# A hybrid decoder layer: the softmax attention's gate projected ahead of the linear attention's values, output sums begun with the softmax attention's part

## The chip, the cores and the metric

One core of a Trainium2 chip runs the whole program. The metric is the device time of one execution in microseconds (us); of several runs the median is given.

## The reference

One decoder layer for 512 prompt tokens and 8 sample tokens (one new token each of 8 running sequences), model width 1024. One input projection `h = x @ w_in` gives nine groups of columns; two mixers work on them side by side:

```python
qa, ka, va, za, ga, qb, kb, vb, gb = split(x @ w_in)      # 256 256 512 16 512 | 512 512 512 512
o_a = gated_linear_attention(qa, ka, va, decay(za))       # 4 heads, state 64 x 128, chunk-wise
o_a = rms_norm(o_a) * gla_norm_g
o_b = dilated_attention(qb, kb, vb, rel_bias)             # 8 heads of 64; windows (128,1),(512,4),(2048,16)
mix = concatenate([o_a * silu(ga), o_b * silu(gb)])       # 512 columns of part a, 512 of part b
y   = mix @ w_out
x_new = layer_norm(ALPHA * x + y) * ln_g + ln_b
```

Sample tokens do the same, with a given state for the linear attention and 1024 cached rows of keys and values each for the softmax attention. Everything is float32. The outputs are the new x, the states and the key and value rows.

## The kernel before, in words

**Numbers.** Each large product is taken as three matmuls of rounded halves: hi·hi, hi·lo, lo·hi (`three`). So each weight group is loaded raw, cast to its half hi on ScalarE (ACT), and subtracted to lo on VectorE (DVE); in the trace these are hi_vb, lo_vb and so on. The names end in parts: `lo1_vb1` is the lo half of load 1 of the second vb group.

**The projections.** The generator `dense()` writes TensorE's (PE) main stream: the projections in the order ka, za, qa, qb, kb, vb, va, ga, gb, and then the output projection. Groups of w_in are 128 columns wide (feature-major result, `feature`) or 256 wide (token-major result, `token`, for vb and va). The list `names` (L493) sets the order in which weights are loaded; the order of the code in `dense()` sets that of the matmuls. Tokens stand as four tiles of 128; u = 0 and 1 are the two halves of 256 tokens, and the first half also carries the 8 sample tokens (264 columns).

**The softmax attention (b).** For each head h and token tile the scores land in banks ps_s (`scores`); `softmax` adds the bias strip and takes the row maximum on DVE (`pr<-ps_s,strip`), the exponential on ACT, the division, then transposes the probabilities on PE into a bank ps_pt, from which ACT writes the half pth and DVE the half ptl (both are `pt` for the first token half). `weighted` multiplies them with the values (vhl) into a bank ps_pv; ACT copies half of it to pvl, and DVE adds both to obT, the output of two heads. Scores need q and k, so they run while vb is projected; products need vb as well.

**The sample tokens of b.** Their logits and probabilities (p_s) are made in small rows; psd_s is a scratch array in DRAM, from which the probabilities come back broadcast as pb. GpSimd (POOL) multiplies the cached values vv by pb, and DVE sums them (`o_pv<-vv`, eight times, once for each sample token).

**Gates and mixing.** `gate_into` takes a gate's projection in its bank through ACT (Exp, Ln, Exp into sg) and one DVE product, `ga<-ps_ga,sg` or `gb<-ps_gb,sg`. `mix_b` multiplies gb by obT and splits the product into mhb (ACT) and mlb (DVE). `mix_a` transposes the linear attention's output on PE into ps_oat, multiplies it with ga (`ga<-ps_oat,gn,ga`) and splits it into mha and mla. `mix_sample` does both for the 8 sample columns.

**The output projection.** `out_first` computes the first token half with the weights stationary, in units of 128 output columns (ps_yf): the first three units all do their k tiles 0 to 3 (part a) first and then 4 to 7 (part b), the other five run one by one. `out_turn` transposes the results back. `out_unit` does the second half (ps_y). Then come residual and LayerNorm.

**What sets the order.** Each task is a Python generator with a priority. `Plan.run` picks, by estimated costs, the operation that can start earliest (the lower priority number at a tie), and writes it to its engine; so the program is one fixed list for each engine, and each engine works its list in order. An operation of a task also waits in the planner for marks (`At`), for slots of a kind (`Need`, table SLOTS, L58) and for PSUM banks (BANKS, L67: d 3 for projections, s 3 for scores, t 2 for transposes). Slots that matter here: g (large tiles, 27), r (raw weights, 2), t1 (4; pvl, sg and other small tiles), ob (5; obT, which may also take a t1 slot as a spare). DMAs go over SyncE's (SP) queue in the order of its list. Each instruction is recorded at L359, in `Plan.issue`, so the profile is read by tile names.

Of the kernel before, what the change touches and what calls it, by code (L numbers as in the profile page):

```python
# [20 lines left out]
P = 128  # L21
# [40 lines left out]
    pt=4,  # L62
    t2=3, st=3,
    pr=4,
    t1=4, ob=5,
    m=6)
BANKS = dict(d=3, s=3, t=2)  # L67

# [295 lines left out]
def trunk(ctx: ExitStack, tc: tile.TileContext, xT, xp, xs, state, ck, cv, w_in, wab, gnorm,  # L364
# [81 lines left out]
    class Group:  # L446
# [11 lines left out]

        def load(self, i):
            raw = yield Need("r", f"raw{i}_{self.name}", [P, self.kk, self.w])  # L460
            rows = self.src[i * self.kk * P:(i + 1) * self.kk * P, self.c0:self.c0 + self.w]
            yield D.dma_start(raw, rows.rearrange("(k p) n -> p k n", p=P))
            raws.append((self, i, raw))
            mark("raw")
# [25 lines left out]
    def w_group(name, i, width=P):  # L490
        return Group(w_in, OFF[name] + i * width, f"{name}{i}_", width)

    names = [("ka", 2, P), ("qa", 2, P), ("qb", 4, P), ("kb", 4, P), ("vb", 2, GW), ("va", 2, GW), ("ga", 4, P), ("gb", 4, P)]  # L493
    groups = {f"{n}{i}": w_group(n, i, w) for n, c, w in names for i in range(c)}
    wo = [Group(w_out, g * 512, f"wo{g}_", 512) for g in range(2)]
    order = [g for k, g in groups.items() if k not in ("ka0", "ka1")] + wo
# [161 lines left out]
    def into(key, own, m, scale):  # L658
# [5 lines left out]
            mark(f"{key}_done")  # L664
        return evac

    def dense():
        for _ in range(N_WARM):
            yield T.matmul(warm_ps, warm[:, :P], warm, start=True, stop=True)
        free(warm_ps)  # L670
        free(warm)

        pk = {}
        for i in range(2):
            for u in range(2):
# [24 lines left out]
        for x in ("qh0", "ql0", "qh1", "ql1"):  # L700
            yield from make(x, Need("g", x, [P, 4, 256], F32R), 4)
        for i in range(4):
            yield from feature(groups[f"qb{i}"], parts("q", q_s, i, 0.125))
        for i in range(4):
            yield from make(f"kp{i}", Need("g", f"kp{i}", [P, 2, 512], F32R), 2)
            yield from feature(groups[f"kb{i}"], parts("k", k_s, i, 1.0))
        for i in range(2):
            for u in range(2):
                yield from make(f"vhl{i}{u}", Need("g", f"vhl{i}{u}", [P, 2, 4, 2, 64], F32R))
            yield from token(groups[f"vb{i}"], *vb_into(i))  # L710
        for u in range(2):
            yield from make(f"va{u}", Need("g", f"va{u}", [P, 2, 512]))
        for i in range(2):
            yield from token(groups[f"va{i}"], *va_into(i))
        for n, own in (("ga", ga_s), ("gb", gb_s)):
            for u in range(2):
                yield from make(f"{n}{u}", Need("g", f"{n}{u}", [P, 4, 256]))
            for i in range(4):
                yield from feature(groups[f"{n}{i}"], gate_into(n, own, i))
        free(*xt)  # L720
        for t in range(TT):
            add(residual(t), 8)
        add(residual_sample(), 8)
        units = [(g, f) for g in range(4) for f in range(2)]
        yield from out_first(*units[:3])
        for x in units[3:]:
            yield from out_first(x)
        for t, c, w in ((2, 0, 512), (2, 512, 512), (3, 0, 512), (3, 512, GW), (3, 768, GW)):
            yield from out_unit(t, c, w)
# [439 lines left out]
    def weighted(h, pi):  # L1169
# [4 lines left out]
            yield At(f"vb{h // 4}{i}", 2)  # L1174
        pth, ptl = B[f"pth{h}{pi}"], B[f"ptl{h}{pi}"]
        if h % 2 == 0:
            yield from make(f"obT{pi}{m}", Need(("ob", "t1"), f"obT{pi}{m}", [P, 256], spare=2))
        else:
            yield At(f"obT{pi}{m}")
        pv = yield bank(("s", "t"), f"ps_pv{h}{pi}")  # L1180
# [230 lines left out]
        if plan.marks[f"mix_b{u}"] == 4:  # L1411
            free(B[f"gb{u}"])

    def mix_sample():
        yield At("ga_s", 4)
        yield At("o_as")
        yield At("mla0")
        gas = ga_s.rearrange("p h b -> p b h")
        yield V.scalar_tensor_tensor(gas, o_as.rearrange("p (b h) -> p b h", h=HA), gn, gas, op0=ALU.mult, op1=ALU.mult)
        yield from split(ga_s, B["mha0"][:, :, GW:], B["mla0"][:, :, GW:])  # L1420
        mark("mix_s")
        yield At("gb_s", 4)
        yield At("o_bs")
        yield At("mlb0")
        yield V.tensor_tensor(gb_s, gb_s, o_bs, op=ALU.mult)
        yield from split(gb_s, B["mhb0"][:, :, GW:], B["mlb0"][:, :, GW:])
        mark("mix_s")


    def ln_rows():  # L1430
# [17 lines left out]
    def out_unit(t, c, w):  # L1448
        u, tl, cs = t // 2, slice((t % 2) * P, (t % 2) * P + P), slice(c % 512, c % 512 + w)
        g = wo[c // 512]  # L1450
        ps = yield bank("d", f"ps_y{t}{c // GW}")
        for k in range(KT):
            yield g.at(k)
            yield At(f"mix_a{u}", t % 2 + 1) if k < 4 else At(f"mix_b{u}{k - 4}")
            mh, ml = (B[f"m{x}{'ab'[k // 4]}{u}"][:, k % 4, tl] for x in "hl")
            hi, lo = g.hi[k][:, cs], g.lo[k][:, cs]
            yield from three(ps[:, :w], k, ((mh, hi), (mh, lo), (ml, hi)))
        add(out_evac(t, c // GW, ps[:, :w]), 2)

    def out_first(*units):  # L1460


        ps = []
        for g, f in units:
            ps.append((yield bank("d", f"ps_yf{g}{f}")))
            yield from out_half(g, f, ps[-1], range(4))
        for (g, f), p in zip(units, ps):
            yield from out_half(g, f, p, range(4, KT))
            add(out_turn(g, f, p), 2)

    def out_half(g, f, ps, ks):
        w, c = wo[g // 2], g % 2 * GW + f * P
        for k in ks:
            yield w.at(k)
            yield At("mix_a0", 2) if k < 4 else At(f"mix_b0{k - 4}")
            yield At("mix_s", 1 + k // 4)
            mh, ml = (B[f"m{x}{'ab'[k // 4]}0"][:, k % 4, :] for x in "hl")
            hi, lo = w.hi[k][:, c:c + P], w.lo[k][:, c:c + P]
            yield from three(ps[:, :TW[0]], k, ((hi, mh), (lo, mh), (hi, ml)))

# [105 lines left out]
    add(sample_v(vnt, "vnt", by_tile(vw_s)), 12)  # L1586
    add(sample_v(vat, "vat", by_tile(vad)), 12)
    add(sample_gla(), 11)
    add(mix_sample(), 16)
    add(ln_rows(), 17)  # L1590
    add(keys_store(), 17.5)
    for pi in range(2):
# [107 lines left out]
```

## Time and profile before

| | us |
|---|---|
| three runs | 293.41, 294.40, 294.72 |
| median | 294.4 |
| the profiled execution | 294.9 |
| its span on the core | 293.1 |
| granted clock of TensorE, mean | 0.984 |

The span is the time from the first to the last instruction that the trace shows. Before about 104 us the projections of ka to kb run; the vb projection and the first products of the softmax attention stand at 104 to 137, the rest of the softmax attention with va and the linear attention beside it at 137 to 202, the gates at 183 to 236, and the output projection from 236 on. A window's row gives, for each engine, its busy us and its instructions in that stretch. A wait `A tile <- B tile` says that engine A stood until B's instruction had written that tile.

### The profile page before, as it was taken

How to read it: one execution, taken by the hardware profiler on the slowest of the kernel's cores; microseconds unless marked ns; L12 is line 12 of the kernel's file. 1: busy time of each engine (PE TensorE's matmuls, PEld its weight loads, DVE VectorE, ACT ScalarE, POOL GpSimd, SP SyncE). 2: the span in 40 equal slices, each digit the busy share in tenths (PEclk: the TensorE clock that was granted, in tenths of full speed). 3: DMA queues.
4: the chain of work that ended last, by engine and by line, in shares of the span. 5: the costliest groups of instructions: out<-in, count | busy, mean ns of one | idle time of the engine just before them, and what ended most of it. 6: DMA issues, size and time to landing. Idle time of an engine off the chain costs nothing.

```text
span 293.1 us, 6910 instructions
## 1 busy us (share of the span) xinstructions
PE 276.3 (94%) x2636; PEld 260.4 (89%) x2636; DVE 228.7 (78%) x562; ACT 167.6 (57%) x463; POOL 57.3 (20%) x74
## 2 busy tenths in 40 slices
PE   7999999999999996999989899998999999999990
PEld 3899999998999995999978799998999999997880
DVE  4746897999799959679869877889899875339855
ACT  4747565356648756466857751789779964111100
POOL 4000001000872238000335535210410000000000
PEclk9999999999999999899999999999999999999996
DMA  6976422236967798148988967924954688650311
GB/s 189 289 199 183 130 74 73 75 83 201 308 189 208 243 246 269 41 129 218 251 187 199 275 161 209 238 75 137 290 151 144 202 269 266 115 173 26 121 74 72
DMA packets 58935, 51.18 MB, mean 175 GB/s; under 512 B 12554, under 2 KB 50196, under 8 KB 58902
## 3 DMA queue, kind: packets, MB, share of 16 engines
q1 hardware_dynamic: 58794, 50.66, 61.4%
q8 instruction: 21, 0.34, 0.5%
q14 instruction: 12, 0.10, 0.1%
q10 hardware_dynamic: 108, 0.07, 0.1%
HBM read 45.17 MB, written 6.03 MB: 175 GB/s over the span
## 4 chain that ended last, share of the span: by engine, by line
PE 71%; DVE 14%; DMA 6%; ACT 5%; issue 2%; SPq 0%; DVEq 0%; ACTq 0%
PE ps_yf L359 8%; PE ps_qb L359 8%; PE ps_gb L359 8%; PE ps_y L359 8%; PE ps_kb L359 4%; DMA strip<-tabr 4%; PE ps_qa L359 4%; PE ps_vb L359 4%; PE ps_vb_f L359 3%; PE ps_ka L359 3%; PE ps_ga L359 3%; DMA x_raw<-in_xT_dram 2%; PE ps_l L359 2%; PE ps_pv L359 2%; PE ps_va L359 2%
## 5 line engine op out<-in xcount | busy, mean ns | idle before, releaser
L359 POOL TENSOR_TENSOR vv<-vv,pb 128x256 f32<-128x256 f32 x32 | 27.9, 901 | 68.0 <-DMA pb<-psd_s 58.7
L359 POOL TENSOR_TENSOR past<-past,qbc 128x256 f32<-128x256 f32 x32 | 25.2, 820 | 43.1 <-DMA past<-in_ck_dram 37.5
L359 ACT ACTIVATE pr<-pr,ms 128x128 f32<-128x128 f32 (+3 forms) x49 | 26.0, 547 | 7.6 <-DVE ms L359 7.2
L359 PE MATMUL ps_pt<-cf,pr 128*128 128x128 f32 x80 | 14.5, 281 | 2.7 <-DVE pt L359 2.3
L359 DVE CUSTOM_DVE_ANT_0 pr<-ps_s,strip 128x128 f32<-128x128 f32 (+3 forms) x32 | 14.2, 478 | 1.0 <-DMA strip<-tabr 1.0
L359 PE MATMUL ps_ka<-xx,hi_ka 128*128 128x264 f32 (+1 forms) x64 | 12.6, 291 | 1.2 <-DVE xx L359 0.7
L359 ACT ACTIVATE sg<-sg 128x264 f32<-128x264 f32 (+1 forms) x32 | 13.3, 416 | 0.5
L359 PEld LDWEIGHTS ps_pt<-cf,pr 128*128 128x128 f32 x80 | 9.4, 142 | 3.7 <-DVE pt L359 2.7
L359 PEld LDWEIGHTS ps_ka<-xx,hi_ka 128*128 128x128 f32 x64 | 10.0, 188 | 2.5 <-DVE xx L359 1.1
L359 ACT COPY feat_y<-ps_yf 128x256 f32<-128x256 f32 x8 | 3.0, 373 | 15.2 <-PE ps_yf L359 15.2
L359 ACT ACTIVATE d<-d 128x512 f32<-128x512 f32 x13 | 7.8, 637 | 6.7 <-DVE d L359 6.7
L359 DVE TENSOR_TENSOR ptl<-ps_pt,pth 128x384 fp32r<-128x384 f32 (+1 forms) x16 | 9.6, 616 | 0.6 <-ACT pth L359 0.6
L359 ACT ACTIVATE rstd<-mv 128x1 f32<-128x1 f32 x4 | 0.7, 199 | 16.3 <-DVE mv L359 16.3
L359 POOL MEMSET att<- 64x512 f32 x2 | 1.0, 522 | 44.8 <-DVE ks L359 44.8
L359 DVE TENSOR_REDUCE o_pv<-vv 128x4 f32<-128x1024 f32 x8 | 9.7, 1209 | 0.0
L359 DVE TENSOR_REDUCE lt<-past 128x16 f32<-128x1024 f32 x8 | 9.6, 1202 | 0.0
L359 DVE TENSOR_TENSOR pt<-ps_pt,pt 128x128 fp32r<-128x128 f32 (+1 forms) x16 | 5.4, 347 | 5.3 <-ACT pt L359 5.3
L359 ACT CAST pth<-ps_pt 128x384 fp32r<-128x384 f32 (+1 forms) x16 | 8.4, 534 | 1.8 <-PE ps_pt L359 1.7
L359 DVE COPY lt<-ps_yf 128x8 f32<-128x8 f32 x6 | 1.0, 166 | 10.7 <-ACT feat_y L359 10.7
L359 PE MATMUL ps_ka<-xx,lo_ka 128*128 128x264 f32 (+1 forms) x32 | 9.1, 286 | 0.0
L359 ACT CAST pt<-ps_pt 128x128 fp32r<-128x128 f32 (+1 forms) x16 | 5.0, 317 | 6.8 <-PE ps_pt L359 6.6
L359 DVE TENSOR_TENSOR d<-b 128x1024 f32<-128x1024 f32 x7 | 8.5, 1217 | 0.0
(536 smaller groups left out, 1105.1 us busy)
## 6 DMA issues: line engine op xcount, KB each, us to landing
past<-in_ck_dram SPq DMA_DIRECT2D x8, 512.0 KB
vv<-in_cv_dram SPq DMA_DIRECT2D x8, 512.0 KB
pb<-psd_s SPq DMA_DIRECT2D x16, 256.0 KB
qbc<-qsd SPq DMA_DIRECT2D x8, 256.0 KB
strip<-tabr SPq DMA_DIRECT2D x8, 256.0 KB
y<-in_xp_dram SPq DMA_DIRECT2D x4, 512.0 KB
x_raw<-in_xT_dram SPq DMA_DIRECT2D x7, 260.0 KB
out_dram<-y SPq DMA_DIRECT2D x3, 512.0 KB
```

Source lines behind the costliest of these rows:

```text
L359: getattr(eng.eng, op.fn)(*op.args, **op.kw)
```

## The change

Five things are changed; what is computed is the same.

1. Slots: t1 has 6 instead of 4, ob 4 instead of 5, and obT takes only ob slots.
2. The projections' order is ka, za, qa, qb, kb, vb, gb, va, ga: gb now stands ahead of va, ga last. The loads of the weights follow. mix_b's steps can so be taken as soon as a pair of heads has its obT.
3. Sums of the output projection begin with part b: k tiles 0 to 3 are now mix_b's, 4 to 7 mix_a's, and w_out's rows are loaded in that order.
4. `out_first` begins with five units of part b, not three of part a, and its banks may come from d or s.
5. `mix_sample` is cut in two, for a and for b.

```diff
-    t1=4, ob=5,
+    t1=6, ob=4,
...
-            rows = self.src[i * self.kk * P:(i + 1) * self.kk * P, self.c0:self.c0 + self.w]
+            k = (i * self.kk + KT // 2 * (self.src is w_out)) % KT
+            rows = self.src[k * P:(k + self.kk) * P, self.c0:self.c0 + self.w]
...
-    names = [... ("vb", 2, GW), ("va", 2, GW), ("ga", 4, P), ("gb", 4, P)]
+    names = [... ("vb", 2, GW), ("gb", 4, P), ("va", 2, GW), ("ga", 4, P)]
...
+    def gates(n, own):
+        for u in range(2):
+            yield from make(f"{n}{u}", Need("g", f"{n}{u}", [P, 4, 256]))
+        for i in range(4):
+            yield from feature(groups[f"{n}{i}"], gate_into(n, own, i))
...
+        yield from gates("gb", gb_s)
         for u in range(2):
             yield from make(f"va{u}", Need("g", f"va{u}", [P, 2, 512]))
         for i in range(2):
             yield from token(groups[f"va{i}"], *va_into(i))
-        for n, own in (("ga", ga_s), ("gb", gb_s)):
-            for u in range(2):
-                yield from make(f"{n}{u}", Need("g", f"{n}{u}", [P, 4, 256]))
-            for i in range(4):
-                yield from feature(groups[f"{n}{i}"], gate_into(n, own, i))
+        yield from gates("ga", ga_s)
...
-        yield from out_first(*units[:3])
-        for x in units[3:]:
+        yield from out_first(*units[:5])
+        for x in units[5:]:
             yield from out_first(x)
...
-            yield from make(f"obT{pi}{m}", Need(("ob", "t1"), f"obT{pi}{m}", [P, 256], spare=2))
+            yield from make(f"obT{pi}{m}", Need("ob", f"obT{pi}{m}", [P, 256]))
...
-            yield At(f"mix_a{u}", t % 2 + 1) if k < 4 else At(f"mix_b{u}{k - 4}")
-            mh, ml = (B[f"m{x}{'ab'[k // 4]}{u}"][:, k % 4, tl] for x in "hl")
+            yield At(f"mix_b{u}{k}") if k < 4 else At(f"mix_a{u}", t % 2 + 1)
+            mh, ml = (B[f"m{x}{'ba'[k // 4]}{u}"][:, k % 4, tl] for x in "hl")
...
-            ps.append((yield bank("d", f"ps_yf{g}{f}")))
+            ps.append((yield bank(("d", "s"), f"ps_yf{g}{f}")))
```

What this does to the engines' lists is seen at three places.

**VectorE while vb is projected.** The names: `pt4`, `pt5`, `pt6` are probabilities of heads 4 to 6 of the first token half, ps_pt their banks; `vhl01` takes the first vb group's result; `obT00` and `obT01` are outputs of heads 0 and 1 and of heads 2 and 3; ln_new, l32, prod and lt belong to the sample logits. Before:

```order
L359 TENSOR_REDUCE lt_82<-past5_1576 128x2x8
L359 TENSOR_TENSOR pt4_1742<-ps_pt41_1767,pt4_1742 128x2x128
L359 TENSOR_TENSOR lo1_vb1__1803<-raw1_vb1__1496,hi1_vb1__1802 128x512 x2
L359 TENSOR_TENSOR vhl01_1579<-ps_vb0_3_1762,vhl01_1579 128x4x64
L359 TENSOR_TENSOR pt5_1746<-ps_pt50_1793,pt5_1746 128x128
L359 TENSOR_TENSOR prod_1719<-q_rows_79,k_rows_1697 32x128
L359 TENSOR_TENSOR lo0_va0__1813<-raw0_va0__1613,hi0_va0__1812 128x512
L359 TENSOR_REDUCE ln_new_1834<-prod_1719 32x2
L359 TENSOR_TENSOR l32_1835<-ln_new_1834,sel_1677 32x64
L359 TENSOR_TENSOR lo0_va0__1813<-raw0_va0__1613,hi0_va0__1812 128x512
L359 TENSOR_TENSOR obT00_1722<-ps_pv00_1723,pvl00_1741 64x256
L359 TENSOR_TENSOR obT00_1722<-ps_pv10_1724,pvl10_1847 64x256
```

The same place now:

```order
L359 TENSOR_TENSOR obT00_1726<-ps_pv00_1727,pvl00_1748 64x256
L359 TENSOR_TENSOR obT01_1729<-ps_pv30_1731,pvl30_1767 64x256
L359 TENSOR_TENSOR vhl01_1579<-ps_vb0_2_1679,vhl01_1579 128x4x64
L359 TENSOR_TENSOR pt4_1749<-ps_pt40_1750,pt4_1749 128x128
L359 TENSOR_REDUCE lt_82<-past5_1576 128x2x8
L359 TENSOR_TENSOR pt4_1749<-ps_pt41_1779,pt4_1749 128x2x128
L359 TENSOR_TENSOR pt5_1754<-ps_pt50_1791,pt5_1754 128x128
L359 TENSOR_TENSOR lo1_vb1__1820<-raw1_vb1__1496,hi1_vb1__1819 128x512
L359 TENSOR_TENSOR vhl01_1579<-ps_vb0_3_1771,vhl01_1579 128x4x64
L359 TENSOR_TENSOR l32_1722<-ln_new_1721,sel_1677 32x64
L359 TENSOR_TENSOR obT00_1726<-ps_pv10_1728,pvl10_1753 64x256
L359 TENSOR_TENSOR pt5_1754<-ps_pt51_1812,pt5_1754 128x2x128
```

Two obT rows have moved ahead of the split of vb1, that split is cut in two halves with rows between, and the split of va0 is gone from here (that of gb0 comes some rows later).

**SyncE's queue after the sample probabilities.** `psd_s` holds them in DRAM, `vv` is the cached values of one sample token, `pb` its probabilities broadcast. Before:

```order
L359 DMA psd_s_90<-p_s_2050 64x256
L359 DMA vv0_2090<-in_cv_dram 128x1024
L359 DMA pb0_2100<-psd_s_90 64x4x256 x2
L359 DMA out_5_dram<-vb_raw_2135 128x256
L359 DMA raw1_va1__2152<-in_w_in_dram 128x4x256
L359 DMA vv1_2144<-in_cv_dram 128x1024
L359 DMA pb1_2177<-psd_s_90 64x4x256
L359 DMA raw0_ga0__2181<-in_w_in_dram 128x8x128
L359 DMA pb1_2177<-psd_s_90 64x4x256
L359 DMA strip51_2234<-tabr_87 128x1x512
```

The same place now:

```order
L359 DMA psd_s_90<-p_s_2034 64x256
L359 DMA vv0_2070<-in_cv_dram 128x1024
L359 DMA out_5_dram<-vb_raw_2094 128x256
L359 DMA pb0_2082<-psd_s_90 64x4x256 x2
L359 DMA vv1_2119<-in_cv_dram 128x1024
L359 DMA pb1_2129<-psd_s_90 64x4x256 x2
L359 DMA raw0_gb3__2152<-in_w_in_dram 128x8x128
L359 DMA out_5_dram<-vb_raw_2181 128x256
L359 DMA raw0_va0__2188<-in_w_in_dram 128x4x256
L359 DMA strip51_2212<-tabr_87 128x1x512
```

vv1 and pb1 have moved ahead of the raw weights that stood between.

**VectorE at the last gate.** `ga_s` and `gb_s` are the sample columns. Before:

```order
L359 TENSOR_TENSOR gb0_3237<-ps_gb3_0_3572,sg_3619 128x256
L359 TENSOR_TENSOR gb_s_86<-ps_gb3_0_3572,sg_3619 128x8
L359 TENSOR_TENSOR gb0_3237<-gb0_3237,obT03_2020 128x256
L359 SCALAR_TENSOR_TENSOR ga_s_85<-o_as_84,gn_68,ga_s_85 128x8x4
L359 TENSOR_TENSOR mlb0_3310<-gb0_3237,mhb0_3309 128x256
L359 TENSOR_TENSOR mla0_3212<-ga_s_85,mha0_3211 128x4x8
L359 TENSOR_TENSOR gb_s_86<-gb_s_86,vnt_80 128x32
L359 TENSOR_TENSOR lo0_wo1__3623<-raw0_wo1__3565,hi0_wo1__3622 128x512
```

The same place now:

```order
L359 TENSOR_TENSOR ga0_3115<-ps_ga3_0_3536,sg_3593 128x256
L359 TENSOR_TENSOR ga_s_85<-ps_ga3_0_3536,sg_3593 128x8
L359 SCALAR_TENSOR_TENSOR ga0_3115<-ps_oat_3620,gn_68,ga0_3115 128x4x128
L359 SCALAR_TENSOR_TENSOR ga_s_85<-o_as_84,gn_68,ga_s_85 128x8x4
L359 TENSOR_TENSOR mla0_3619<-ga0_3115,mha0_3618 128x4x128
L359 TENSOR_TENSOR lo0_wo1__3599<-raw0_wo1__3528,hi0_wo1__3598 128x512
L359 SCALAR_TENSOR_TENSOR ga0_3115<-ps_oat_3630,gn_68,ga0_3115 128x4x128
L359 TENSOR_TENSOR lo0_wo1__3599<-raw0_wo1__3528,hi0_wo1__3598 128x512
```

Before, mix_b's last step followed the last gate; now it is both steps of mix_a for the first token half, and the first splits of wo1 stand among them.

More of the change, by code (lines that the diff above doesn't have):

```diff
@@ L491, in w_group @@
         return Group(w_in, OFF[name] + i * width, f"{name}{i}_", width)
-    names = [("ka", 2, P), ("qa", 2, P), ("qb", 4, P), ("kb", 4, P), ("vb", 2, GW), ("va", 2, GW), ("ga", 4, P), ("gb", 4, P)]
+    names = [("ka", 2, P), ("qa", 2, P), ("qb", 4, P), ("kb", 4, P), ("vb", 2, GW), ("gb", 4, P), ("va", 2, GW), ("ga", 4, P)]
     groups = {f"{n}{i}": w_group(n, i, w) for n, c, w in names for i in range(c)}
@@ L1412, in mix_b, with mix_sample_a @@
             free(B[f"gb{u}"])
-    def mix_sample():
+    def mix_sample_a():
         yield At("ga_s", 4)
@@ L1420, in mix_sample, with mix_sample_b @@
         yield from split(ga_s, B["mha0"][:, :, GW:], B["mla0"][:, :, GW:])
-        mark("mix_s")
+        mark("mix_sa")
+    def mix_sample_b():
         yield At("gb_s", 4)
@@ L1426, in mix_sample @@
         yield from split(gb_s, B["mhb0"][:, :, GW:], B["mlb0"][:, :, GW:])
-        mark("mix_s")
+        mark("mix_sb")
     def ln_rows():
@@ L1474, in out_half @@
             yield w.at(k)
-            yield At("mix_a0", 2) if k < 4 else At(f"mix_b0{k - 4}")
-            yield At("mix_s", 1 + k // 4)
-            mh, ml = (B[f"m{x}{'ab'[k // 4]}0"][:, k % 4, :] for x in "hl")
+            yield At(f"mix_b0{k}") if k < 4 else At("mix_a0", 2)
+            yield At(f"mix_s{'ba'[k // 4]}")
+            mh, ml = (B[f"m{x}{'ba'[k // 4]}0"][:, k % 4, :] for x in "hl")
             hi, lo = w.hi[k][:, c:c + P], w.lo[k][:, c:c + P]
@@ L1588, in trunk @@
     add(sample_gla(), 11)
-    add(mix_sample(), 16)
+    add(mix_sample_a(), 16)
+    add(mix_sample_b(), 16)
     add(ln_rows(), 17)
```

## The prediction

> **What bounds the kernel now.** I read the busy times of the page first, then a table of windows cut at the places where TensorE pauses, then the waits inside those windows, and last the timeline of VectorE (DVE) around the longest pause. The page's busy row:
>
> ```profile
> PE 276.3 (94%) x2636; PEld 260.4 (89%) x2636; DVE 228.7 (78%) x562; ACT 167.6 (57%) x463; POOL 57.3 (20%) x74
> ```
>
> PE carries the run, and the change leaves its matmuls as they are, in kind and in number. So only the time in which PE stands, or runs slowly, can come or go. The windows show where that is (per engine: busy us and instructions; then PE's granted clock, the DMA share and GB/s):
>
> ```profile
> 113.40:116.60 3.20, 0.65 (x5) 0.25 (x3) 3.04 (x9) 1.84 (x7) 3.20 (x5) 1.00 0.64 196
> 116.60:120.00 3.40, 3.40 (x17) 3.40 (x17) 1.87 (x4) 0.84 (x3) 1.21 (x2) 0.50 0.45 157
> 120.00:137.00 17.00, 17.00 (x143) 15.90 (x142) 14.25 (x40) 12.35 (x33) 0.00 (x0) 1.00 0.42 119
> 137.00:165.00 28.00, 26.03 (x215) 23.75 (x213) 23.23 (x59) 19.54 (x50) 12.00 (x15) 1.00 0.95 220
> 165.00:183.00 18.00, 17.67 (x166) 17.24 (x168) 13.38 (x27) 8.92 (x21) 8.34 (x11) 1.00 0.74 207
> 183.00:202.00 19.00, 18.53 (x161) 17.75 (x157) 16.72 (x58) 15.59 (x66) 2.83 (x4) 1.00 0.54 126
> 202.00:236.00 34.00, 33.54 (x305) 33.21 (x305) 31.23 (x76) 28.68 (x76) 4.70 (x4) 1.00 0.70 203
> 236.00:285.30 49.30, 49.11 (x336) 44.80 (x334) 29.76 (x85) 10.90 (x35) 0.00 (x0) 1.00 0.50 152
> ```
>
> Three places: a pause of 3.20 − 0.65 = 2.55 us at 113.4 to 116.6, with 3.4 us at clock 0.50 behind it; 28.00 − 26.03 = 2.0 us in 137 to 165; and about 0.5 us each near 202. The output projection from 236 on has no gap worth a term. Their names, from the waits (of 110 to 120, then 137 to 166, then 183 to 203: total, times, longest):
>
> ```profile
> PE ps_pt L359 <- DVE pt L359: 2.1, 1, 2.1
> PE ps_pt L359 <- DVE obT L359: 0.4, 1, 0.4
> ACT pvl L359 <- DVE obT L359: 0.8, 1, 0.8
> ...
> PE ps_turn L359 <- ACT feat L359: 1.3, 1, 1.3
> PE ps_va L359 <- DVE ms L359: 0.9, 1, 0.9
> ...
> PE ps_ga L359 <- DVE ga L359: 0.8, 1, 0.8
> ```
>
> The long pause is DVE working through its queue while PE needs a transpose bank (ps_pt). The timeline of DVE (start, duration) shows in which order:
>
> ```profile
> 109.61 1.29 DVE L359 TENSOR_TENSOR lo_vb__1803<-raw_vb__1496,hi_vb__1802 128x512 fp32r<-128x512 f32 x2
> 110.86 0.42 DVE L359 TENSOR_TENSOR vhl<-ps_vb,vhl 128x256 fp32r<-128x256 f32 x1
> 111.54 0.29 DVE L359 TENSOR_TENSOR pt<-ps_pt,pt 128x128 fp32r<-128x128 f32 x1 [0.26 <-ACT pt L359]
> 111.75 0.85 DVE L359 TENSOR_TENSOR prod<-q_rows,k_rows 32x128 f32<-32x128 f32 x1
> 112.53 0.67 DVE L359 TENSOR_TENSOR lo_va__1813<-raw_va__1613,hi_va__1812 128x512 fp32r<-128x512 f32 x1
> 113.13 0.27 DVE L359 TENSOR_REDUCE ln_new<-prod 32x2 f32<-32x128 f32 x1
> 113.44 0.45 DVE L359 TENSOR_TENSOR l<-ln_new,sel 32x64 f32<-32x64 f32 x1
> 113.81 0.67 DVE L359 TENSOR_TENSOR lo_va__1813<-raw_va__1613,hi_va__1812 128x512 fp32r<-128x512 f32 x1
> 114.41 0.85 DVE L359 TENSOR_TENSOR obT<-ps_pv,pvl 64x256 f32<-64x256 f32 x2
> 115.29 0.42 DVE L359 TENSOR_TENSOR pt<-ps_pt,pt 128x256 fp32r<-128x256 f32 x1
> ```
>
> Between 111.75 and 114.4 DVE does sample logits and weight splits for va0, none of which PE needs now. The four products ps_pv wait behind that, in banks that the score transposes also draw from: obT runs only at 114.41 and the pt that PE waits for at 115.29.
>
> **The change part by part.**
>
> *A. Slots t1 4 to 6, gb0 in place of va0 (the vb stage).* pvl and the gates' sg share t1, and obT may no longer take a spare t1 slot, so the copies pvl start without the wait of 0.8. In the changed order two obT rows stand ahead of all splits of vb1 and gb0, so two of the four product banks come back early. What the pause costs today: 2.55 us idle, and the slow stretch. Its price, from the same projection at both clocks:
>
> ```profile
> 110.25:113.39 3.14, 3.14 (x24) 2.92 (x24) 0.00 (x0) 0.00 (x0) 1.00 0.95 330
> 116.88:119.67 2.79, 2.79 (x12) 2.79 (x13) 0.00 (x0) 0.00 (x0) 0.50 0.45 154
> ```
>
> A vb matmul takes 3.14/24 = 0.13 us at clock 1.00 and 2.79/12 = 0.23 at 0.50: 17 matmuls in the slow window lose 17 × 0.10 = 1.7. Together 4.2. What stays: the last six matmuls of the first vb1 turn need the second half of lo1_vb1. Between the sample reduce lt (ending near 110) and that half stand, by the durations above, pt 0.42, pt 0.29, a split 0.65, vhl 0.42, l 0.45, obT 0.43, pt 0.42, pt 0.29, a vb_raw copy (0.42, taken as vhl) and the split's second half 0.65: 4.4, so it ends near 114.4. PE reaches it at 113.4 at the earliest, where the pause begins now, and by my count at 113.8: 0.6 lost. Another 0.6 I put on a turn of sample features that waits for DVE behind score rows. Rest 1.2, in two pieces. The pause now is 2.55 and was followed by the slow clock; half of that in one piece I take not to be. **Gain 4.2 − 1.2 = 3.0**, bounds 0 (the pause keeps its length under another name) and 4.2.
>
> [...]
>
> *B. The softmax stage, 137 to 183.* Here the gb projections and their evacuations move in, and va, with its splits and copies, moves behind. What comes along is three ACT steps and one DVE product per gate half, and mix_b's rows as soon as an obT is ready:
>
> ```profile
> L359 DVE TENSOR_TENSOR gb<-ps_gb,sg 128x256 f32<-128x256 f32 x8 | 3.3, 418 | 0.0
> L359 DVE TENSOR_TENSOR gb<-gb,obT 128x256 f32<-128x256 f32 x8 | 3.4, 422 | 0.0
> L359 DVE TENSOR_TENSOR mlb<-gb,mhb 128x256 fp32r<-128x256 f32 x8 | 3.3, 418 | 0.3 <-ACT mhb L359 0.3
> ```
>
> All together 3.3 + 3.4 + 3.3 = 10.0 us of DVE. In 137 to 183 DVE is busy 23.23 + 13.38 = 36.6 of 46, so 9.4 free; with PE's matmuls of the gates the stage grows by some 4 us. 46.6 of 50: it fits, barely. The named waits there, 1.3 + 0.9 = 2.2, are waits on DVE and on ACT behind DVE; va's go, new ones of the same kind come (a score row behind mix_b rows). I found 0.5 to 1 by hand and take 2.2 again, since a queue that is 93% full makes waits that hand-following misses: **0**, bounds +2.2 (all gone) and −2.4.
>
> The lower bound is contention between DVE and POOL, which also works in this stage. Splits of one shape without and with a POOL row beside them, and POOL's own row without and with DVE:
>
> ```profile
> 132.74 0.69 DVE L359 TENSOR_TENSOR lo_va__2120<-raw_va__1815,hi_va__2119 128x512 fp32r<-128x512 f32 x1
> 157.70 2.25 DVE L359 TENSOR_TENSOR lo_va__2489<-raw_va__2152,hi_va__2488 128x512 fp32r<-128x512 f32 x2
> ...
> 150.22 2.81 POOL L359 TENSOR_TENSOR vv<-vv,pb 128x256 f32<-128x256 f32 x4 [8.26 <-DVE ptl L359]
> 157.52 4.96 POOL L359 TENSOR_TENSOR vv<-vv,pb 128x256 f32<-128x256 f32 x4 [4.50 <-DMA pb<-psd_s]
> ```
>
> Two splits took 2.25 where 1.38 was due, and POOL 4.96 where 2.81 was: about 0.4 more for each DVE row that meets POOL. The 16 mix_b rows have two SBUF inputs each; they move from 202 to 236, where POOL is busy 4.70 of 34, to 137 to 183, where it is 12.00 + 8.34 = 20.3 of 46. 16 × 0.44 × 0.35 = 2.4, if all of it lands on PE.
>
> [...]
>
> *C. The ga stage, 183 to 236.* Now 0.8 of PE's waiting is on the gate product ga, behind mix_b rows and splits. With mix_b gone I leave 0.3: **gain 0.5**, bounds +0.8 and −1 (va's copies now stand in the same place).
>
> *D. The output projection.* It begins with k from the b part for five units, then their a halves. At the start only mix_b is needed, long done. The a part is due after five b halves, 5 × 12 = 60 matmuls:
>
> ```profile
> 236.26 7.50 PE ps_yf L359 x58
> ...
> L359 DVE SCALAR_TENSOR_TENSOR ga<-ps_oat,gn,ga 128x512 f32<-128x512 f32 x4 | 2.9, 746 | 0.2
> L359 DVE TENSOR_TENSOR mla<-ga,mha 128x512 fp32r<-128x512 f32 x4 | 3.7, 921 | 0.0
> ```
>
> 60 × 7.50/58 = 7.8 us of cover. In it DVE does, up to mix_a0's end, the last ga product 0.42, two ga products 1.5, two mla 1.8 and two splits of wo1 1.4: 5.1, with ACT's casts between them. It is covered, but with the cover gone (three units: 4.7) it would cost some 0.4 and more. wo1 arrives inside the same stretch. **0**, bounds 0 and −2.
>
> Sum: 3.0 + 0 + 0.5 + 0 = 3.5. The profiled execution took 294.9 (span 293.1 and 1.8 around it); 294.9 − 3.5 = 291.4. The median of the runs shown, 294.4, lies 0.5 lower, so the forecast is **290.9**.
>
> **The rivals.** A difference under 0.5%, 1.5 us, a measurement of this kernel can't tell from no change.
>
> *The filler hides everything.* Waits A, B and C all go: 4.2 + 2.2 + 0.8 − 0.7 for one short wait that stays = 6.5; 294.4 − 6.5 = 287.9. For it: gb needs only x, so PE has work that waits for nothing. Against: DVE at 93% in the stage.
>
> *The vb pause only changes its name.* PE waits for lo1_vb1 or a pt row for over 2 us and the clock halves again. DVE's share of 113.4 to 116.6, 3.04 of 3.20, speaks for it; that two obT now stand ahead, against. A gives 0 to 1, C 0.5: 293.5.
>
> *DVE held at o_pv1, slower.* DVE runs in order, and in the changed order the reduce o_pv of the second sample token stands ahead of the score rows of the heads 4 and 5. It needs POOL's product vv1, which needs pb1, which comes back from psd_s over SyncE's queue. Now:
>
> ```profile
> 131.08 0.53 SPq L359 DMA_DIRECT2D psd_s<-p_s  x1
> ```
>
> vv1 ends at 150.22 + 2.81 = 153.0, 22.0 after that issue. In the changed order raw1_va1 and raw0_ga0, 0.52 MB each, no longer stand ahead of pb1's second half; at 220 GB/s they are 4.8 us, so vv1 ends 17.2 to 22.0 after the issue. DVE's 44 rows between p_s and o_pv1 are, by the durations of their kinds, 20.3 in sum and 17.2 net of overlaps. So DVE waits 0 to 4.8 us. Behind it on DVE stand score rows, and PE waits for these once the matmuls released before, about 6 × 0.13 = 0.8, are spent: up to 4.0 idle and then the slow clock, 1.7: 290.9 + 5.7 = **296.6**. It is slower than now from a wait of DVE above 3.5 or so.
>
> **How the numbers follow.** Forecast 0.46, own range 289.0 to 292.9 (A by ±1.2, B's contention). Hides everything 0.12, 287.3 to 288.9. The pause stays 0.22, 292.9 to 295.5. DVE held 0.20, 294.9 to 297.5, nearly all above 295.9. The range from 287.7 to 296.6 leaves out about a third of the second and half of the last case, some 0.14. Faster by over 0.5%, under 292.9: 0.46 + 0.12 = 0.58. Within: 0.22 and a little of the last, 0.23. Slower, above 295.9: 0.19.
>
> **What would show it.** Right: no wait of PE above 1 us between 108 and 120 and no window there at clock 0.50; in the softmax stage PE's waits sum to about 2; no wait on mla at the switch from b to a halves. Wrong: a wait of PE of over 2 us on pt, lo_vb or ms with clock 0.50 behind it; DVE idle before o_pv; mix_b rows of 0.8 instead of 0.42; a wait of PE on lo_wo or mla after the first 60 ps_yf matmuls.

## The result, and the profile after

The changed kernel took 290.5 us (median of 290.04, 290.11, 290.89 and 291.47); the kernel before, run again beside it, 294.56 (median of four, 293.41 to 295.62). The ratio is 0.9867, with a 95% interval of 0.982 to 0.991. The kernel before scatters by some 4 us from run to run, and by more than 1 us from chip to chip (medians of 293.1, 293.25 and 294.5 on three), so the experiments below are compared by their ratio to the kernel before on the same chip; their medians are over undisturbed executions alone, which leaves out, among others, two executions of the kernel before that took 929 us.

The profiled execution took 290.1, its span is 288.3: 4.8 less than the span before. Its windows, cut so that each stage of before has its counterpart (columns as in the table of windows of before):

```profile
104.00:125.00 21.00, 19.88 (x166) 18.45 (x165) 18.36 (x46) 13.06 (x38) 8.41 (x10) 1.00 0.70 211
137.00:183.00 46.00, 44.40 (x369) 42.17 (x368) 42.20 (x94) 33.24 (x87) 19.65 (x24) 1.00 0.94 215
183.00:235.00 52.00, 51.70 (x478) 50.32 (x477) 40.35 (x122) 37.14 (x126) 4.50 (x6) 1.00 0.68 189
240.00:280.30 40.30, 40.05 (x263) 35.83 (x261) 23.93 (x70) 5.97 (x23) 0.00 (x0) 1.00 0.41 117
```

The first of these windows in the kernel before, for its clock:

```profile
104.00:125.00 21.00, 18.45 (x142) 17.47 (x141) 15.12 (x40) 11.28 (x34) 8.25 (x11) 0.92 0.61 182
```

PE's waits in the changed kernel from 100 to 232, all that are named:

```profile
PE ps_pt L359 <- DVE ptl L359: 0.9, 1, 0.9
PE ps_vb_f L359 <- DVE lo_vb__1820 L359: 0.7, 1, 0.7
PE ps_pt L359 <- DVE pt L359: 0.4, 1, 0.4
PE ps_pt L359 <- DVE pr L359: 0.3, 1, 0.3
PE ps_ort L359 <- DVE o_r L359: 0.3, 1, 0.3
PE ps_pv L359 <- DVE ms L359: 0.3, 1, 0.3
```

The wait of 2.1 on pt is gone, and no wait reaches 1 us. Set against the kernel before, stage by stage:

| stage | lost before | lost after | gain |
|---|---|---|---|
| vb (104 to 125) | idle 2.55, clock 0.08 x 21 = 1.7 | idle 1.12, clock full | 3.1 |
| softmax (137 to 183) | idle 1.97 + 0.33 = 2.30 | 1.60 | 0.7 |
| ga stage (to the output projection) | 0.47 + 0.46 = 0.93 | 0.30 | 0.6 |
| output projection | 0.19 | 0.25 | −0.1 |

Together 4.3 of 4.8. The rest was there before 104: the second turn of the vb result starts at 100.38 before and at 99.97 after (0.4), in a part whose code is the same, so I take it for scatter.

VectorE's timeline in the vb stage shows the new order at work: an obT early, the split of lo_vb in two, and PE waiting only for its second half:

```profile
107.12 0.42 DVE L359 TENSOR_TENSOR obT<-ps_pv,pvl 64x256 f32<-64x256 f32 x1 [0.58 <-ACT pvl L359]
109.89 0.69 DVE L359 TENSOR_TENSOR lo_vb__1820<-raw_vb__1496,hi_vb__1819 128x512 fp32r<-128x512 f32 x1
111.29 0.42 DVE L359 TENSOR_TENSOR obT<-ps_pv,pvl 64x256 f32<-64x256 f32 x1
112.72 1.10 DVE L359 TENSOR_TENSOR lo_vb__1820<-raw_vb__1496,hi_vb__1819 128x512 fp32r<-128x512 f32 x1
```

### The profile page after: what moved, and what is told of

Same layout as the page of the kernel before. It is cut to its first block, busy times and chain, and to the rows that moved or that the text cites. A ratio compares the mean times of both kernels' runs of the same rounds, so it can differ in the third digit from the quotient of the medians.

```text
span 288.3 us, 6893 instructions
## 1 busy us (share of the span) xinstructions
PE 275.0 (95%) x2636; PEld 259.7 (90%) x2636; DVE 228.9 (79%) x563; ACT 164.2 (57%) x462; POOL 57.2 (20%) x74
## 4 chain that ended last, share of the span: by engine, by line
PE 66%; DVE 20%; ACT 5%; DMA 5%; issue 3%; SPq 0%; DVEq 0%
PE ps_qb L359 8%; PE ps_y L359 8%; PE ps_kb L359 7%; PE ps_ga L359 6%; PE ps_yf L359 4%; PE ps_qa L359 4%; PE ps_va L359 4%; PE ps_vb L359 4%; PE ps_ka L359 3%; PE ps_vb_f L359 3%; DMA raw_wo__3728<-in_w_out_dram 2%; DMA raw_ka<-in_w_in_dram 2%; PE ps_l L359 2%; PE ps_va_f L359 2%; DVE pr L359 2%
## 5 line engine op out<-in xcount | busy, mean ns | idle before, releaser
L359 POOL TENSOR_TENSOR vv<-vv,pb 128x256 f32<-128x256 f32 x32 | 27.0, 873 | 45.7 <-DMA pb<-psd_s 38.7
L359 POOL TENSOR_TENSOR past<-past,qbc 128x256 f32<-128x256 f32 x32 | 26.0, 849 | 42.0 <-DMA past<-in_ck_dram 36.5
L359 PE MATMUL ps_pt<-cf,pr 128*128 128x128 f32 x80 | 13.8, 277 | 1.7 <-DVE ptl L359 0.9
L359 PE MATMUL ps_ka<-xx,hi_ka 128*128 128x264 f32 (+1 forms) x64 | 13.6, 309 | 0.4 <-DVE xx L359 0.3
L359 PEld LDWEIGHTS ps_ka<-xx,hi_ka 128*128 128x128 f32 x64 | 11.1, 206 | 1.4 <-DVE xx L359 0.8
L359 DVE TENSOR_TENSOR obT<-ps_pv,pvl 64x256 f32<-64x256 f32 x16 | 6.6, 414 | 3.3 <-ACT pvl L359 3.1
L359 DVE TENSOR_TENSOR xx<-x_raw,xx 128x520 fp32r<-128x520 f32 (+2 forms) x9 | 5.7, 640 | 3.8 <-ACT xx L359 3.8
L359 ACT COPY pvl<-ps_pv 64x256 f32<-64x256 f32 x16 | 5.5, 369 | 5.5 <-PE ps_pv L359 5.4
```

The source lines that it names most:

```text
L359: getattr(eng.eng, op.fn)(*op.args, **op.kw)
```

## The experiments

**The slots alone, as the change has them.** The kernel before with

```diff
-    t1=4, ob=5,
+    t1=6, ob=4,
...
-            yield from make(f"obT{pi}{m}", Need(("ob", "t1"), f"obT{pi}{m}", [P, 256], spare=2))
+            yield from make(f"obT{pi}{m}", Need("ob", f"obT{pi}{m}", [P, 256]))
```

> The kernel before with the slots alone changed (t1 6, ob 4, obT from ob only). Theory (the gain is the pause at the vb projection, and the slots end it): the early copies pvl and the early obT come back with the slots alone, the pause of 2.55 us and the 3.4 us at clock 0.50 go, the waits of the softmax and gate stages (2.2 and 0.8) stay: 3 us under the kernel before, about 291.5. Rival (the gain is the gate moved ahead): 294 to 295, no difference.

Measured: 293.75 against 293.25, ratio 1.0025 (0.999 to 1.006): no gain. But the pause is gone. The waits of PE from 100 to 235:

```profile
PE ps_gb L359 <- DVE gb L359: 3.7, 2, 2.2
PE ps_ga L359 <- DVE ga L359: 0.9, 1, 0.9
PE ps_vb_f L359 <- DVE lo_vb__1820 L359: 0.7, 1, 0.7
PE ps_pt L359 <- DVE pt L359: 0.2, 1, 0.2
```

What was won at the vb projection is waited away on gb in the gate stage. VectorE's timeline suggests why. In the kernel before, three of the four outputs of the second token half are written from 137.6 to 165.3, ahead of the first ga product at 186.5, and the fourth at 218.4. Here all four come behind the first gb product (194.0), from 200.5 to 237.0. The four ob slots hold the first half's outputs until mix_b frees them, and mix_b needs gb, which comes last. So this run doesn't price the pause; the one with a single slot more, below, is meant to.

**The order and the sums without the slots.** The changed kernel with those two lines as before.

> The changed kernel with the old slots (t1 4, ob 5, obT with a spare t1). Theory: the pause comes back with the slow clock behind it, 3 us over the changed kernel, about 293.5 to 294, and a window at clock 0.50 near 116. Rival (the gate moved ahead brings the gain): 290.5 to 291.5 and no window at a low clock.

Measured: 294.57 against 293.25, ratio 1.0046 (1.001 to 1.008). The pause is back, with the slow clock behind it, as expected:

```profile
113.80:116.40 2.60, 0.77 (x5) 0.38 (x3) 2.48 (x9) 1.97 (x7) 2.60 (x4) 0.96 0.82 233
116.40:119.80 3.40, 3.40 (x17) 3.40 (x18) 1.98 (x4) 0.87 (x3) 1.44 (x3) 0.53 0.46 149
```

The moved gate and the new order of the sums gain nothing without the slots, then. They are even a little slower than the kernel before.

**Three units in place of five.**

```diff
-        yield from out_first(*units[:5])
-        for x in units[5:]:
+        yield from out_first(*units[:3])
+        for x in units[3:]:
...
-            ps.append((yield bank(("d", "s"), f"ps_yf{g}{f}")))
+            ps.append((yield bank("d", f"ps_yf{g}{f}")))
```

> The changed kernel, the output projection begun with three units of part b in place of five, banks of d alone. Cover ahead of the first matmul of part a 36 x 0.13 = 4.7 us in place of 7.8, and 5.1 us of VectorE's work due in it. Theory: a wait on mla of 0.4 to 1, the time 0.4 to 1 over the changed kernel, 291 to 291.5. Rival (the five units are what makes the gain): 292.5 or more.

Measured: 289.45 against 293.25, ratio 0.9872 (0.984 to 0.991), the same as the changed kernel within the intervals, and from 225 to 250 PE waits 0.3 for o_r and nothing for mla. Five units aren't needed. In the timeline, the last write of mla for the first token half and PE's first matmul of part a:

```profile
233.52 0.69 DVE L359 TENSOR_TENSOR mla<-ga,mha 128x512 fp32r<-128x512 f32 x1
235.87 0.29 PE L359 MATMUL ps_yf<-mha,hi_wo__3464 128*128 128x264 f32 x1
```

mla is ready at 234.21, 1.7 us before it is read.

**The sums begun with part a.** The changed kernel with part a first in `out_first` and `out_unit`, three units, and w_out's rows in the old order; gb still ahead of va. One line of the edit shows it:

```diff
-            yield At(f"mix_b0{k}") if k < 4 else At("mix_a0", 2)
+            yield At("mix_a0", 2) if k < 4 else At(f"mix_b0{k - 4}")
```

> The changed kernel with the output sums begun with part a as before (three units, w_out's rows in the old order), the gate gb still ahead of va and ga last. Theory: with no cover the first matmuls wait for mix_a's work after the last ga gate, 4 to 5 us on VectorE, and the clock halves behind it (1.7): 5 to 6.5 over the changed kernel, 295.5 to 297; the order of sums by itself gains nothing against the kernel before, but the moved gate needs it. Rival (the order of the sums hides nothing, since PE has other work): under 292.

Measured: 293.29 against 293.25, ratio 1.0012 (0.998 to 1.004): all of the gain is lost, 1.4% by the ratios against three units in the same set of runs, 3.8 us by the medians. PE's waits from 225 to 245:

```profile
PE ps_oat L359 <- DVE ga L359: 1.4, 1, 1.4
PE ps_yt L359 <- ACT feat_y L359: 0.8, 1, 0.8
PE ps_yf L359 <- DVE mla L359: 0.5, 1, 0.5
PE ps_ort L359 <- DVE o_r L359: 0.3, 1, 0.3
```

The wait at the seam is there, smaller than the 4 to 5 us that I expected and, in the profiled execution, without a slow clock (1.00 from 225 to 240); the first three, 2.7, explain most of the 3.8.

**The changed kernel once more.**

> The changed kernel once more, beside the kernel before on the same chip, since the kernel before scatters from 290.7 to 294.8 in the runs so far. Theory: 0.985 to 0.990 of the kernel before, 3 to 4.5 us. Rival (part of the first difference was scatter): 0.993 or more.

Measured: 289.6 against 294.5, ratio 0.9834 (0.979 to 0.988). The gain holds on another chip; it was 1.3% in the first set and 1.7% in this one.

**One more slot t1 and nothing else.** This prices the pause without the loss of an ob slot:

```diff
-    t1=4, ob=5,
+    t1=5, ob=5,
```

> The kernel before with one more slot t1 (5 in place of 4) and nothing else; obT keeps its five slots and the spare. The list of VectorE then has the two early obT rows ahead of the splits of vb1, as the changed kernel has. Theory (the slots alone gained nothing because four slots ob hold the products of the second token half back until gb, which stood last there, and not because the pause is worth nothing): the pause and its slow clock go, the second half's obT stay at their old place: 2 to 3 us under the kernel before. Rival (VectorE is full in the gate stage in any case, so what is gained at the pause waits there): within 1 us of the kernel before, with waits on gb or ga of 2 us and more.

Measured: 294.1 against 294.5, ratio 0.9977 (0.994 to 1.001). My expectation fell. The time is the rival's, within 1 us of the kernel before, but the waits on gb or ga that the rival named aren't there. In the vb stage the kernel lost 0.38 in place of 2.55, at full clock; but at the end of the gate stage there is now this (windows, then PE's waits from 202 to 236):

```profile
104.00:125.00 21.00, 20.62 (x171) 19.10 (x170) 18.65 (x49) 13.87 (x40) 9.60 (x12) 1.00 0.68 203
202.00:235.00 33.00, 30.36 (x275) 29.63 (x274) 31.09 (x79) 26.93 (x75) 4.80 (x4) 1.00 0.75 212
```

```profile
PE ps_yf L359 <- ACT mha L359: 1.6, 1, 1.6
PE ps_ort L359 <- DVE o_r L359: 1.1, 1, 1.1
```

The output projection begins with part a, whose sample columns wait for the linear attention's sample output o_r. In the kernel before, the same cast of mha ended just as PE came to it:

```profile
235.93 0.21 ACT L359 CAST mha<-ga_s 128x32 fp32r<-128x32 f32 x1
236.19 0.39 PE L359 MATMUL ps_yf<-mha,hi_wo__3385 128*128 128x264 f32 x1
```

235.93 + 0.21 = 236.14, and PE starts at 236.19, so the seam from the gates to the output projection cost nothing there, by 0.05 us. In the kernel with five slots PE is done with the gates 4.9 us earlier, at 231.3, and waits. But that is not the only difference: PE's list has changed as well. The sample output o_r is made from the matmuls ps_og, and the gate matmuls ps_gb that stand between ps_og and the first ps_yf cover the steps from one to the other. Those matmuls alone, in the kernel before and then with five slots (behind a stretch and its length, PE's busy time and count come first):

```profile
229.97:236.19 6.22, 6.22 (x50) 6.04 (x50) 0.91 (x3) 0.76 (x2) 1.00 0.75 234
228.29:234.28 5.99, 3.06 (x24) 2.85 (x24) 0.74 (x3) 0.76 (x2) 1.00 0.96 274
```

Fifty matmuls, 6.2 us, cover the chain in the kernel before, and 24 of them, 3.1 us, here. Whether the seam shows because PE comes earlier or because the chain stands later in PE's list, no run separates.

**GpSimd only writes.** The changed kernel's lists, with GpSimd's multiply replaced as it is issued:

```diff
+        if eng.name == "POOL" and op.fn == "tensor_tensor" and op.args[0].tensor.name.startswith("vv"):
+            eng.eng.memset(op.args[0], 0.25)
+            self.issued += 1
+            return
```

> The changed kernel, its lists of instructions the same row for row, but GpSimd writes a constant into vv in place of multiplying vv by pb, so the softmax attention's part of the sample tokens is not computed. It shows what the meeting of VectorE and GpSimd costs. Theory: the 16 rows of mix_b fall from 0.56 to about 0.42 (2.3 us of VectorE less), little of it on PE, whose idle in 137 to 183 is 1.6 now: 0.3 to 1 under the changed kernel. Rival (all of it lands on PE): 2 us or more under it.

Measured: 288.5 against 294.5, ratio 0.9806 (0.977 to 0.985); the changed kernel had 0.9834 in the same set, so 1.1 us by the medians, with intervals that overlap. That is a little over the 0.3 to 1 that I expected, and well under the rival's 2. The profiles are clearer: the rows of mix_b in the changed kernel, then here (where a recorded line has number L363), then the softmax stage here:

```profile
L359 DVE TENSOR_TENSOR gb<-gb,obT 128x256 f32<-128x256 f32 x8 | 4.5, 573 | 0.0
L359 DVE TENSOR_TENSOR mlb<-gb,mhb 128x256 fp32r<-128x256 f32 x8 | 4.4, 556 | 0.5 <-ACT mhb L359 0.5
```

```profile
L363 DVE TENSOR_TENSOR gb<-gb,obT 128x256 f32<-128x256 f32 x8 | 3.3, 420 | 0.0
L363 DVE TENSOR_TENSOR mlb<-gb,mhb 128x256 fp32r<-128x256 f32 x8 | 3.3, 420 | 0.5 <-ACT mhb L363 0.5
```

```profile
137.00:183.00 46.00, 46.00 (x393) 44.85 (x392) 40.40 (x100) 35.43 (x93) 4.96 (x19) 1.00 1.05 208
```

The move costs VectorE 4.5 + 4.4 − 6.6 = 2.3 us, and with GpSimd writing a constant PE has no idle at all in a stage where it had 1.60 in the first profile of the changed kernel and 0.95 in the profile of this set. Writing a constant also frees GpSimd from waiting for pb; but in the changed kernel VectorE's waits in this stage name ACT alone (1.3, 1.0, 0.8 and 0.4 in all), so a late product of GpSimd is not what is missing here. The same row of mix_b took 0.57 us beside GpSimd's multiply and 0.42 where GpSimd wrote a constant; whether its reads count or the time it is busy, 19.65 us and then 4.96 in this stage, no run separates.

**Two holds at the vb stage.** The changed kernel's lists, and ahead of the second half of lo1_vb1 two reduces on VectorE:

```diff
+        if eng.name == "DVE" and op.args[0].tensor.name.startswith("lo1_vb1"):
+            self.hold += 1
+            if self.hold == 2:
+                for _ in range(2):
+                    eng.eng.tensor_reduce(self.scratch, self.long, axis=AX.XY, op=ALU.add)
```

> The changed kernel, its lists the same, with two reduces of 128x1024 (about 1.2 us each, of a constant, result unused) put on VectorE ahead of the second half of lo1_vb1, so that PE's pause of 0.7 there becomes one of about 3. Theory (a pause of 2 to 2.6 us is followed by a stretch at clock 0.50, as in the kernel before and with the old slots): 2.2 for the pause and 1.7 for the clock, 3.5 to 4 over the changed kernel, and a window at 0.50. [...]

Measured: 293.2 against 294.5, ratio 0.9961 (0.993 to 0.999), 1.3% by the ratios or 3.6 us by the medians over the changed kernel in the same set; expected were 3.5 to 4. The pause and the clock behind it:

```profile
113.90:117.10 3.20, 0.33 (x3) 0.18 (x2) 3.17 (x4) 0.89 (x3) 3.00 (x5) 1.00 0.12 42
117.10:120.50 3.40, 3.40 (x18) 3.40 (x19) 3.31 (x6) 0.44 (x2) 0.36 (x1) 0.55 0.71 180
```

So a pause of 2.9 on this spot, put back into the changed kernel, takes three quarters of its gain (3.6 of 4.9) away.

**Is VectorE full at the seam?** The kernel with five slots, the product of mix_b cut to 8 columns as it is issued:

```diff
+        if eng.name == "DVE" and op.fn == "tensor_tensor" and op.args[2].tensor.name.startswith("obT"):
+            op.args = [x[:, :8] for x in op.args]
```

> The kernel before with five slots t1, its lists row for row those of that kernel, but the eight products gb x obT on VectorE take 8 columns of 256, so most of part b is left unmultiplied: about 0.35 less each, 2.8 us less on VectorE, all in the gate stage. Theory (with the pause gone VectorE is what the seam to the output projection waits for: it was busy 31.1 of 33 us in 202 to 235, and PE waited 2.7 there for o_r and mha): the waits at the seam fall by 2 to 2.8 and the time to 2 to 2.8 under the kernel with five slots, 0.988 to 0.991 of the kernel before. Rival (the seam waits on the sample tokens' chain by its own latencies, whatever VectorE has to do): within 0.5 of the kernel with five slots, 0.996 to 0.999.

Measured: 292.85 against 293.1, ratio 0.9997 (0.996 to 1.003). The eight products took 1.2 us in place of 3.3, so 2.1 us less and not the 2.8 that I had expected. The wait on mha is 1.6 as before, that on o_r 0.5 in place of 1.1. My theory that VectorE is simply full there fell: 2.1 us of work less moved the seam by 0.6. What is left is the chain of short steps of the sample tokens, passed between VectorE, ACT and PE, and its place in PE's list, which is the same as with five slots (24 gate matmuls behind ps_og). No run takes the chain itself out, so that it is the cause is argued.

**One slot, and the sums begun with part b.** The kernel with five slots, part b first in three units, w_out's rows to match, `mix_sample` cut in two; va, ga, gb in the old order.

> The kernel before with five slots t1 and the output sums begun with part b (three units, w_out's rows in that order, mix_sample cut in two), the projections still in the order va, ga, gb. Theory (VectorE full in the gate stage): the wait on mha goes, but one on mlb of the last gate takes its place, and since that is 1 to 2 us the kernel stays 0.993 to 0.998 of the kernel before. Rival (only the sample part of mix_a held the seam, so the order of the sums and one slot bring the gain, and gb need not move): 0.988 or less.

Measured: 291.9 against 293.1, ratio 0.9948 (0.990 to 0.9995). PE's waits from 202 to 250:

```profile
PE ps_yf L359 <- ACT mhb L359: 2.0, 1, 2.0
PE ps_yf L359 <- DVE lo_wo__3835 L359: 0.8, 1, 0.8
```

As expected, the wait on part a became one on part b: gb is now the last gate, and the first sums need its sample columns, whose steps on ACT and VectorE follow that gate's matmuls. But most of the 2.0 is not the length of these steps. ACT's list has a cast of w_out ahead of the last gate's sg, and ACT stood for its load:

```profile
228.55 0.62 ACT L359 CAST hi_wo__3558<-raw_wo__3506 128x512 fp32r<-128x512 f32 x1 [1.66 <-DMA raw_wo__3506<-in_w_out_dram]
```

With five slots alone the same cast had waited 0.28. About a third of the changed kernel's gain is there by the middle of the interval, which reaches from almost none to two thirds.

**A version that may be best.** Three units, five slots t1 and five ob, in the changed kernel.

> A version that may be best: the changed kernel with three units of part b first, five slots t1 and five ob. Theory: as the changed kernel with three units, 0.983 to 0.988 of the kernel before, and PE's idle in 137 to 183 a little less, since one more obT can stand ready. Rival (four ob with gb ahead hold nothing, so the slot is worth nothing, and the later early obT costs): 0.988 to 0.990.

Measured: 291.95 against 293.1, ratio 0.996 (0.992 to 0.9997): less than the changed kernel gained, and outside both ranges; the rival was only the nearer one. PE's idle in 137 to 183 was 2.30, where the kernel with three units had 1.03, and PE waited 1.5 on o_r and 0.4 on mha at the seam, and 0.6 twice on gb rows. Five and five slots put the sample chain late in PE's list again: 33 gate matmuls stand behind ps_og and none behind ps_ort, the transpose of o_r, where the kernel with three units has 54 and 10. So six t1 and four ob are a part of the gain, by intervals that don't meet; no run shows which of their effects it is. I found no version that clearly beats the changed kernel; three units equal it.

**One hold.** As with two, but one reduce.

> The changed kernel with one reduce of 128x1024 (1.2 us) ahead of the second half of lo1_vb1 on VectorE, not two. PE's pause there becomes 1.8 to 2.0 and the one of 0.4 behind it goes. Theory (a pause of 2.9 halved the clock, one of 0.7 didn't; with the old slots about 2.0 did): the clock halves, 0.8 + 1.7 = 2.5 over the changed kernel, 0.993 of the kernel before. Rival (the length has to be above some 2.5): 0.8 over it, clock at 1.00, 0.987.

Measured: 292.6 against 293.1, ratio 0.9969 (0.992 to 1.002). The pause of the vb stage came in two pieces: PE waited 1.26 on pt, did five matmuls, and waited 1.61 on the second half of lo1_vb1. The granted clock stayed at 1.00 through it and behind it, so in the profiled execution the theory fell, with 2.87 of idle in all. It did not fall for every execution: seven of the twelve had a granted clock of 0.982 to 0.989, five of 0.990 to 0.995, and the profiled one is of the second kind (the last section says what the two mean). The time can't be read as the price of the hold alone, since the profile has another pause, at 177, of a kind that I had forecast as a rival:

```profile
178.51 1.22 DVE L364 TENSOR_REDUCE o_pv<-vv 128x4 f32<-128x1024 f32 x1 [2.69 <-POOL vv L364]
```

```profile
177.00:180.20 3.20, 0.86 (x8) 0.66 (x6) 1.69 (x5) 0.59 (x2) 1.48 (x3) 1.00 0.87 165
```

VectorE stands 2.69 in order at o_pv for GpSimd's product, and PE stands 2.34 with it.

## Why the prediction was right, point by point

The forecast of 290.9 stands against 290.5, and the signs and most sizes of its terms hold. That the two are so close is partly luck: the terms measured in the profile sum to 4.3 and not to 3.5, and the second set gave 4.9. The reasoning behind them, that the terms can be added up one by one, does not.

**A, the vb pause, forecast 3.0.** Measured 3.1: rest 1.12 where 1.2 was forecast, no slow clock. The first rest is what I named, 0.7 on lo_vb for the forecast 0.6; the second is 0.4 on pt and not a turn of sample features. That the slots bring it and not the moved gate is shown: one slot removes the pause, the moved gate without slots doesn't. But I wrote its price as if it would come out at the end by itself. One slot more won it at the vb stage, and 0.2%, within noise, was left of it in the time. And 1.7 of it is the price of a slow stretch that the profiled execution of the kernel before had, and by the granted clocks about three of four executions of it.

**B, the softmax stage, forecast 0.** Measured 0.7 in this execution. The contention that I had as the lower bound, 2.4 us of VectorE, came, 2.3; PE paid some 1.0 to 1.6 for it (1.1 by the times with GpSimd writing a constant, 0.95 and 1.60 by the idle in two profiles), and the removed waits brought more. VectorE was 42.2 of 46, 92%.

**C, the ga stage, forecast 0.5.** Measured 0.6.

**D, the output projection, forecast 0.** Measured −0.1, so the sum is right, and here lies the step that failed: "with the cover gone (three units: 4.7) it would cost some 0.4 and more". With three units it cost nothing; with part a first 3.8, the whole gain. I had taken the order of the sums for a change whose price is zero if it is hidden. It is rather the condition of A: where nothing covers the steps from the last gate, or those of the sample chain, to the first sum, PE waited 1.9 to 2.7 us at the seam (2.7 with five slots, 2.0 with part b first there, of which a late load has the larger share, 1.9 on ga and mla with part a first). The kernel before had the sample chain covered by the gate matmuls behind it, with 0.05 us to spare.

**The rival of the held o_pv** did not happen here. In the changed kernel the sample probabilities go out and the second product ends as follows:

```profile
125.75 0.51 SPq L359 DMA_DIRECT2D psd_s<-p_s  x1
...
139.79 3.04 POOL L359 TENSOR_TENSOR vv<-vv,pb 128x256 f32<-128x256 f32 x4 [2.89 <-DMA pb<-psd_s]
...
145.84 1.21 DVE L359 TENSOR_REDUCE o_pv<-vv 128x4 f32<-128x1024 f32 x1
```

vv1 ends 142.83 − 125.75 = 17.1 after the issue, the low end of my 17.2 to 22.0, and VectorE reaches o_pv at 20.1, the sum of 20.3 without overlaps. Both came out at the harmless end of what I had given for them. The wait is real all the same: with one hold VectorE stood 2.69 at the o_pv of another sample token.

**The rival that the filler hides everything** is what is seen when GpSimd writes a constant: no idle in the stage, 288.5. GpSimd's multiply beside VectorE's rows is what kept the changed kernel from it, as far as that one run shows.

## What to carry to other kernels

Where one engine carries the run, a pause removed early can be worth nothing until the next meeting point has slack: look for what ended just in time before (here a cast that ended 0.05 us ahead of its reader), see whether the new list still covers it, and cover it where it doesn't. Parts of a change that each gain nothing alone may gain together, so undo them one at a time from the whole as well as adding them to the old; slots alone, the moved gate and new sums without slots, and the gate with the old sums all came out at the kernel before, and all together at 1.3% and 1.7% less. And when slots are taken from one kind of tile for another, ask in the list who frees them: with gb last, four slots held the attention's second half until the gates. Last, a profile is one execution: see by the granted clocks of the others whether its slow stretches are theirs too, before they go into a sum.

## What the runs showed of the hardware

The length of a pause did not decide whether the clock was halved behind it. Idle of 2.55 in a window of 3.2 (the kernel before), 1.83 in 2.6 (the old slots) and 2.87 in 3.2 (two holds) had a stretch at about 0.5 behind it: 0.50, 0.53 and 0.55 as the means of the next 3.4 us. Idle of 2.04 in 2.6 (the slots alone, at 221.6), 2.64 in 3.2 (the seam of the kernel with five slots) and 2.34 in 3.2 (one hold, at 177) had none, nor had the two pieces of 2.87 together in the vb stage with one hold. The windows of these four, each with what came behind it:

```profile
221.60:224.20 2.60, 0.56 (x5) 0.32 (x4) 2.60 (x5) 2.58 (x9) 1.46 (x2) 1.00 0.29 93
224.20:227.60 3.40, 3.13 (x24) 2.92 (x25) 3.35 (x11) 2.16 (x5) 1.81 (x3) 1.00 0.25 93
```

```profile
231.20:234.40 3.20, 0.56 (x4) 0.26 (x3) 3.04 (x11) 2.84 (x9) 0.00 (x0) 1.00 1.03 273
234.40:238.00 3.60, 3.60 (x30) 3.57 (x30) 2.46 (x8) 1.77 (x4) 0.00 (x0) 1.00 1.00 377
```

```profile
177.00:180.20 3.20, 0.86 (x8) 0.66 (x6) 1.69 (x5) 0.59 (x2) 1.48 (x3) 1.00 0.87 165
180.20:184.00 3.80, 3.59 (x32) 3.62 (x33) 2.28 (x5) 2.45 (x7) 1.33 (x2) 1.00 1.07 217
112.00:116.30 4.30, 1.75 (x13) 1.33 (x12) 3.44 (x7) 3.29 (x8) 3.80 (x6) 1.00 0.54 184
116.30:120.00 3.70, 2.95 (x21) 2.53 (x21) 3.70 (x7) 0.58 (x3) 3.29 (x3) 1.00 0.57 151
```

What did decide is not shown: no run moved one and the same pause in time.

Nor do the executions of one kernel agree, so the same kernel may or may not pay. Of the profiled executions, those with a slow stretch in the middle had a mean granted clock of 0.984 to 0.989 (the kernel before 0.984, the old slots 0.985, two holds 0.989) and those without one 0.990 to 0.995. By that mark, an estimate, 64 of 85 executions of the kernel before in the sets of the experiments had such a stretch, and one of ten of the changed kernel in its two sets. With five slots it was nine of twelve, though the profiled execution had none: there the pause of the vb stage is gone, and the one at the seam may pay for the clock in its place, which would account for a time that hardly moved; those executions have no trace, so that is my estimate.
